# The first MLP of a two-layer block: both phases in a written order on all engines, weight differences kept in DRAM, row sums and row low parts on GpSimd

## The chip, the cores and the metric

The kernel runs on one core of one Trainium2 chip, as one launch. The metric is the device time in microseconds (us). The core has five engines: TensorE (PE; its weight loads are listed as PEld), VectorE (DVE), ScalarE (ACT), GpSimd (POOL) and SyncE (SP), which issues most of the DMAs. A difference under about 0.5% can't be told from none for this kernel.

## The reference, cut to what matters

Two layers over 512 latent tokens and 256 context tokens of width 1024. Layer 0 mixes tokens by pooling, layer 1 by attention; after each comes an MLP. The change is in the MLP of layer 0, which runs over all 768 tokens:

```python
def sq_relu_mlp(h, w_in, w_out):
    return jnp.square(jax.nn.relu(h @ w_in)) @ w_out

m_lat = sq_relu_mlp(modulate(rms_norm(x, g_mlp_pre[i]), sh2, sc2), w_mlp_in[i], w_mlp_out[i])
x = x + gt2 * rms_norm(m_lat, g_mlp_post[i])
```

`w_in` is 1024 x 4096, `w_out` 4096 x 1024, all float32. The context tokens go through the same weights with their own shift, scale and gate. Shifts, scales and gates of a layer come from `silu(cond) @ w_ada + b_ada`.

## The kernel before

**High and low parts.** A float32 product is made from three matmuls on rounded operands: high by high, high by low, low by high. The high part is a rounding copy on ACT (`sc.copy`), the low part a subtraction on DVE. Each operand therefore costs an ACT copy and a DVE subtraction ahead of its matmuls.

**First phase, class `Seven` (L819).** The hidden dimension of 4096 is cut into 16 groups of 256. Groups 2 to 15 are computed by a scheme of seven products in place of eight for a product of 2 x 2 blocks (Winograd's form of Strassen's scheme). The block sums of the rows are made once (`sums`), those of the weights for each group by `weights_sums` (L762), as six steps: casts on ACT, differences and low parts on DVE. A group's seven products are seven chains of 12 matmuls (128 x 128 by 128 x 384). Between the chains, banks of PSUM are copied by ACT to seed other sums, two DVE additions close the second half, and at the end two relus and two squares on ACT write the group's hidden rows into one of two buffers in `acc` (`hiddens`). `run(behind)` issues the pieces of other work (the next group's weight steps, the dots, the row sums) behind each chain.

**Row sums, `left_sums` (L981).** After each pair of groups, four sums of 768 elements per partition are made of their hidden rows on DVE, and seven tensors are written to `lefts` in DRAM through POOL's DMA queue. They are the left operands of the second phase. The hiddens of groups 14 and 15 are written to `ends` in DRAM.

**Dots.** Six tables of layer 1's and 0's conditioning are computed on DVE: a raw block of `w_ada` (1 MB) is loaded and multiplied with a broadcast row, with the sum in the accumulator (`ada_dot`, L343, 128 x 1024 elements). There are 24 blocks, 12 of them for two condition vectors (four dots), 12 for one (two dots). `ask` loads a block and queues its dots. The first phase takes 14 blocks; two go into the second phase; the last eight (`lone`) run in the stage behind the MLP's end, among the projections of the attention (`last0`).

**Second phase, `halves_` (L1054).** The seven-product scheme again, now on pairs of groups: 7 pairs, 7 products each, 49 products. A product is three row tiles of six matmuls (128 x 128 by 128 x 512), accumulated in PSUM over the 7 pairs. The products are grouped in passes, `PASSES = ((5, 3), (6, 4), (0, 1), (2,))`: a pass goes over all pairs for its one or two products, then `take` adds the banks to the result in `acc`. `load(j)` fetches weights and the row tensor of a product four ahead, `prepare(j)` makes weight differences and high and low parts two ahead. Products 3 to 6 need a difference of weight quarters; product 5 needs two, and product 3 starts from it.

**Order.** `TC_OPTS` has the build's planner order each engine's instructions by its own time estimates. `keep_in_program_order` pins an instruction to the written order of its engine. `Kept` is a wrapper that pins everything that an engine issues while its flag is set. Before, the matmuls of both phases are pinned (`mm`), the other engines are planned.

**Behind the MLP.** `finish` adds the products of groups 14 and 15 directly, then come norms, projections to keys, values and queries (`project`, L1380; `head_norm`, L1396 to L1410), the attention, and layer 1's MLP (`mlp1`).

Of the kernel before, what the change touches and what calls it, by code (L numbers as in the profile page):

```python
# [32 lines left out]
LATER, KEPT = 10, 8  # L33
# [65 lines left out]
def backbone(ctx: ExitStack, tc, x, ctx_in, w_ada, w_pool, w_qkv, g_q, g_k, w_o, w_mlp_in,  # L99
             w_mlp_out, vecs, rope, band, out):  # L100
    nc = tc.nc
    ordered, mixed = [False], [False]
    sy, gp = nc.sync, nc.gpsimd
# [31 lines left out]
    ends = dram.tile([P, 2, 2 * TOK], F32, name="ends")  # L135
# [676 lines left out]
    placed = [False]  # L812

    def mm(*args, **kw):
        z = te.matmul(*args, **kw)  # L815
        if placed[0]:
            tc.keep_in_program_order(z)

    class Seven:  # L819
# [3 lines left out]
        def chain(self, bank, n, start, stop):  # L823
            (wH, wL), (aH, aL) = self.products[n]
            for k in range(4):
                for m, (w, a) in enumerate(((wH, aH), (wH, aL), (wL, aH))):
                    mm(bank, w[k], a[k], start=start and k == 0 and m == 0, stop=stop and k == 3 and m == 2,
                       skip_group_check=True)

        def run(self, behind):  # L830
# [4 lines left out]
            for z in (b, c) if self.fresh else ():  # L835
                mm(z, wH[0], aH[0], start=True, stop=True, skip_group_check=True)
# [105 lines left out]
    def out_mm(i, parts, t, cols=HALVES):  # L942
# [12 lines left out]
        for n, h in order:  # L955
            a, f, w = seq[n]
            mm(pss[h][:, 0:cols[h][1]], a[:, f, ts_], w[:, f, cols[h][0]:sum(cols[h])],
               start=(n == 0 and not seeded[t]), stop=(n == len(seq) - 1), skip_group_check=seeded[t])
# [24 lines left out]
    def left_sums(p, even, odd):  # L983
# [3 lines left out]
        def one(n, d, a, b, op):  # L987
            ve.tensor_tensor(out=d, in0=a, in1=b, op=op)
# [16 lines left out]
    PASSES = ((5, 3), (6, 4), (0, 1), (2,))  # L1005

    def mlp0(inner, order, last, before_last):
# [18 lines left out]
        due = left_sums(0, early, hiddens[1])  # L1026
        sum_banks(True)
        placed[0] = True
        for g in range(2, NG):
            seven = Seven(products, hiddens[g % 2], (g + 1) % 2, g < 4)  # L1030
            pieces = []
            if g < NG - 1:
                steps, products = weights_sums(g + 1, raw)
                pieces += steps
                if g < NG - 2:
                    raw = raw_load(w_mlp_in[0, g + 2])
            if asked:
                pieces += asked.pop(0)
            if g % 2 == 0:
                pieces = due + pieces  # L1040
# [4 lines left out]
            for f in pieces[(7 * n + 3) // 7:]:  # L1045
                f()
            if g >= 2 * PAIRS:
                gp.dma_start(two(ends[:, g % 2]), hiddens[g % 2])
            elif g % 2:
                due = left_sums(g // 2, *hiddens)  # L1050
            if g == 4:
                head_gains()
        halves_(before_last)

    def halves_(before_last):
        todo = [(ps, p, n) for ps in range(len(PASSES)) for p in range(PAIRS) for n in PASSES[ps]]
        f, slots = S["f"], lambda z, w, n: [z[:, w * i:w * i + w] for i in range(n)]
        right = [f[:, 0:2048], f[:, 3584:5632]] + slots(ra, 2048, 6)
        left = [f[:, 2048:3584], rb[:, 0:1536]] + slots(f, 1536, 5) + slots(rb1, 1536, 2)
        uheld[0].close()  # L1060
        wide = uheld[0].enter_context(tc.tile_pool(name="wide", bufs=1)).tile([P, 8192], F32, name="wide")
        full = slots(wide, 2048, 4)
        arows = [slots(acc[:, 4 * TOK:], TOK, 4), slots(wide[:, 4096:], TOK, 5)]
        raws, sums_, ops, araw = {}, {}, {}, {}

        def home(slots, j):
            return slots[j] if j < 2 else slots[2 + (j - 2) % (len(slots) - 2)]

        def load(j):
            ps, p, n = todo[j]  # L1070
            raw = lambda: rawp.tile([P, 2048], F32, tag="raw", name="raw")
            if n == PASSES[ps][0]:
                f2 = lambda z: z.rearrange("p (f n) -> p f n", f=2)
                src = [f2(w_mlp_out[0, 2 * p + u]) for u in range(2)]
                z0 = full[(ps + p) % 2] if ps < 3 else raw()
                arow = z0[:, 1024:1024 + TOK]
                if ps == 3:
                    z0 = f2(z0[:, 0:1024])
                    sy.dma_start(z0, src[1][:, :, 512:])
                    raws[ps, p] = None, None, None, z0  # L1080
                elif ps == 2:
                    z0 = f2(z0)
                    for u in range(2):
                        sy.dma_start(z0[:, :, 512 * u:512 * u + 512], src[u][:, :, 0:512])
                    raws[ps, p] = z0[:, :, 0:512], None, z0[:, :, 512:], None
                else:
                    z0, z1 = f2(z0), f2(raw() if ps else full[2 + p % 2])
                    sy.dma_start(z0, src[0])
                    c = 512 if ps else 0
                    sy.dma_start(z1[:, :, c:], src[1][:, :, c:])  # L1090
                    raws[ps, p] = z0[:, :, 0:512], z0[:, :, 512:], z1[:, :, 0:512], z1[:, :, 512:]
            if ps < 3:
                z = arows[ps > 0]
                arow = z[(j + 4) % len(z)]
            araw[j] = arow
            sy.dma_start(arow, lefts[:, p, n])

        def prepare(j):
            ps, p, n = todo[j]
            b11, b12, b21, b22 = raws[ps, p]  # L1100
            tt = lambda d, a, b, op=ALU.subtract: ve.tensor_tensor(out=d, in0=a, in1=b, op=op)  # L1101
            if n in (0, 1, 2):
                b = (b11, b21, b22)[n]
            elif n == 3:
                b = sums_.pop(p)
                tt(b, b, b21)
            else:
                b = two(work_tile())
                tt(b, *((b12, b11), (b22, b12), (b22, b12))[n - 4])
                if n == 5:  # L1110
                    tt(b, b, b11, ALU.add)
                    sums_[p] = b
            r, l = home(right, j), home(left, j)
            wH, wL, aH, aL = two(r[:, 0:1024]), two(r[:, 1024:2048]), two(l[:, 0:TOK]), two(l[:, TOK:2 * TOK])
            sc.copy(wH, b)
            tt(wL, b, wH)
            a = two(araw.pop(j))
            sc.copy(aH, a)
            tt(aL, a, aH)
            ops[j] = wH, wL, aH, aL  # L1120

        where = lambda q, h, c: accv[:, 2 * q + h, 512 * c:512 * c + 512]
        add = lambda d, a, b, op=ALU.add: ve.tensor_tensor(out=d, in0=a, in1=b, op=op)

        def take(n, q, ps):
            c11, c12, c21, c22 = (where(q, h, c) for h in range(2) for c in range(2))
            if n == 5:
                sc.copy(c12, ps)
# [729 lines left out]
```

## Time and profile before

| what | us |
|---|---|
| median of 3 runs (1171.29 to 1175.4) | 1171.42 |
| the profiled execution | 1177.28 |
| its span, first to last instruction | 1175.5 |
| PE busy in the span (95%) | 1117.8 |
| DVE busy (79%) | 933.7 |
| ACT busy (53%) | 622.7 |
| POOL busy (9%) | 103.4 |

The profile is one execution. A row of a group gives the line, engine and operation, the tiles written and read, shapes and count, then the busy time and the mean duration in ns, then the engine's idle time ahead of it and what ended it. A row of a timeline gives start, duration, engine, line and operation, and in brackets the idle time before it and who ended that. PE's matmuls overlap: a row's duration is longer than the distance to the next start, so starts tell more than durations. A helper that records operations for its callers shows as one line, so L95 and L815 stand for many places; tile names tell them apart (`psin` first phase, `pso` second).

### The profile page before, as it was taken

What the parts mean: (1) busy time and instruction counts of PE and PEld (TensorE: products, weight loads), DVE (VectorE), ACT (ScalarE), POOL (GpSimd) and SP (SyncE); (2) the same over time, 40 slices, a digit from 0 to 9 for tenths busy, and PEclk for the clock granted to TensorE, in tenths of its full rate; (3) what the DMA queues carried; (4) which work ended last, traced back from release to release, by engine and by line L of the source; (5) the groups of instructions that cost most, each with busy time, mean ns of one, the idle gap of its engine ahead of it and who ended that gap; (6) DMA issues with size and microseconds to landing.
All of it is one profiled execution on the core that took longest, in us unless ns stands there. A gap on an engine that the chain in (4) does not pass through costs nothing. (4 is left out here: it accounts for less than half of the span.)

```text
span 1175.5 us, 15873 instructions
## 1 busy us (share of the span) xinstructions
PE 1117.8 (95%) x6030; PEld 971.2 (83%) x6030; DVE 933.7 (79%) x1332; ACT 622.7 (53%) x1038; POOL 103.4 (9%) x164
## 2 busy tenths in 40 slices
PE   7799799999979999999999899999999999999997
PEld 6479798999977778888887789998988888888886
DVE  5488888899859898757588889868687679778876
ACT  6387454555544454444385267762676346535523
POOL 1050111111100000000131310001100000000001
PEclk9799899999999999999999999999999999999999
DMA  9893576666699899627424602104434223214212
GB/s 371 287 386 130 188 242 216 209 223 221 230 354 354 305 387 351 206 88 258 160 90 151 243 1 72 37 9 189 154 115 152 76 95 144 108 37 143 108 33 112
DMA packets 48877, 212.62 MB, mean 181 GB/s; under 512 B 7104, under 2 KB 10000, under 8 KB 32160
## 3 DMA queue, kind: packets, MB, share of 16 engines
q1 hardware_dynamic: 43920, 190.76, 45.1%
q0 software_dynamic: 4880, 20.84, 4.6%
q8 instruction: 47, 0.77, 0.3%
q14 instruction: 30, 0.25, 0.1%
HBM read 183.40 MB, written 28.19 MB: 180 GB/s over the span
## 5 line engine op out<-in xcount | busy, mean ns | idle before, releaser
L815 PE MATMUL pso<-ra,sums 128*128 128x512 f32 x630 | 146.7, 393 | 4.7 <-DVE ra L1101 4.1
L815 PEld LDWEIGHTS pso<-ra,sums 128*128 128x128 f32 x630 | 119.1, 190 | 31.2 <-DVE ra L1101 5.4
L683 PE MATMUL psin<-ra,rb 128*128 128x512 f32 (+1 forms) x310 | 87.8, 360 | 0.0
L1256 PE MATMUL pso<-units,pairs 128*128 128x512 f32 x336 | 82.7, 389 | 0.0
L683 PE MATMUL psin<-ra 128*128 128x512 f32 (+1 forms) x256 | 76.5, 376 | 0.0
L1256 PEld LDWEIGHTS pso<-units,pairs 128*128 128x128 f32 x336 | 63.1, 188 | 13.1
L343 DVE CUSTOM_DVE_ANT_0 waste<-raw,crow 128x1024 f32<-128x1024 f32 x56 | 68.3, 1219 | 6.3 <-DMA raw<-in_w_ada 5.9
L815 PE MATMUL psin<-ra,units 128*128 128x384 f32 x340 | 65.9, 343 | 6.2 <-ACT work L694 6.2
L243 POOL TENSOR_SCALAR ms<-ss 128x1 f32<-128x1 f32 x15 | 9.7, 645 | 685.6 <-ACT junk L230 665.6
L1260 DVE TENSOR_TENSOR acc<-acc,pso 128x512 f32<-128x512 f32 x72 | 48.6, 681 | 26.3 <-PE pso L1256 26.3
L815 PEld LDWEIGHTS psin<-ra,units 128*128 128x128 f32 x340 | 61.7, 195 | 6.5 <-ACT work L694 6.5
L683 PEld LDWEIGHTS psin<-ra,rb 128*128 128x128 f32 x310 | 55.6, 189 | 8.7
L815 PE MATMUL psin<-sums,units 128*128 128x384 f32 x336 | 60.8, 334 | 0.9 <-ACT psin L838 0.9
L815 PEld LDWEIGHTS psin<-sums,units 128*128 128x128 f32 x336 | 58.4, 188 | 1.2 <-ACT psin L838 1.2
L683 PE MATMUL psin<-rb,rb 128*128 128x512 f32 (+1 forms) x155 | 55.9, 362 | 0.6 <-DVE rb L1740 0.6
L1380 PE MATMUL psq<-units,ra 128*128 128x512 f32 x216 | 53.8, 400 | 0.9 <-DVE rb L1480 0.9
L683 PEld LDWEIGHTS psin<-ra 128*128 128x128 f32 x256 | 47.1, 188 | 8.7
L815 PE MATMUL pso<-ra,rb 128*128 128x512 f32 x216 | 50.1, 390 | 0.0
L1380 PEld LDWEIGHTS psq<-units,ra 128*128 128x128 f32 x216 | 41.0, 193 | 9.8 <-DVE rb L1480 1.3
L683 PE MATMUL psin<-rb,ra 128*128 128x512 f32 (+1 forms) x128 | 48.1, 376 | 0.0
L815 PEld LDWEIGHTS pso<-ra,rb 128*128 128x128 f32 x216 | 40.5, 188 | 8.6 <-DVE ra L1101 0.3
L986 POOL DMA_DIRECT2D lefts<-acc x48 | 30.1, 627 | 189.3 <-ACT psin L838 108.3
(342 smaller groups left out, 2692.4 us busy)
## 6 DMA issues: line engine op xcount, KB each, us to landing
raw<-in_w_ada SPq DMA_DIRECT2D x48, 1024.0 KB, 7.4
raw<-in_w_mlp_in SPq DMA_DIRECT2D x32, 1024.0 KB, 5.3
wide<-in_w_mlp_out SPq DMA_DIRECT2D x21, 1024.0 KB, 7.4
lefts<-acc POOLq DMA_DIRECT2D x48, 384.0 KB, 6.2
raw<-in_w_mlp_out SPq DMA_DIRECT2D x18, 1024.0 KB, 5.2
wide<-lefts SPq DMA_DIRECT2D x28, 384.0 KB, 6.3
raw<-in_w_mlp_out SPq DMA_DIRECT2D x14, 512.0 KB, 6.4
wide<-in_w_mlp_out SPq DMA_DIRECT2D x14, 512.0 KB, 6.0
```

What stands on the lines that cost most here:

```text
L243: gp.tensor_scalar(out=ms[:, 0:1], in0=ss[:, parts - 1:parts], scalar1=rest, scalar2=EPS, op0=ALU.add, op1=ALU.add)
L343: ve.tensor_tensor_reduce(out=spare, in0=raw[:, D * b:D * b + D], in1=rows[c], scale=1.0, scalar=0.0, op0=ALU.mult, op1=ALU.add, accum_out ...
L683: te.matmul(ps[:, bank, o:o + ln], w[:, k, fs], rhs, start=start, stop=(k == KT - 1 and n == 2), skip_group_check=len(ks) < KT or self.paired)
L815: z = te.matmul(*args, **kw)
L986: keep = lambda n, z: gp.dma_start(two(lefts[:, p, n]), z)
L1256: te.matmul(ps, a, w, start=(m == 0), stop=(m == len(seq) - 1))
L1260: ve.tensor_tensor(out=M[n][:, t], in0=M[n][:, t], in1=ps, op=ALU.add)
L1380: te.matmul(ps, a[:, k, sl], w[:, k % 4, :], start=(k == 0 and n == 0), stop=(k == KT - 1 and n == 2))
```

## The change

- All five engines are pinned in both phases: SP and POOL are wrapped by `Kept` as well, and `pin` sets all flags. The pieces are dealt out by `(n*z + 6)//7` in place of `(n*z + 3)//7`.
- `left_sums` runs on POOL right after an odd group, not on DVE in the next one.
- `Seven` uses the other group of four PSUM banks for even and odd groups.
- `halves_` becomes the class `Halves`. Its first four loads and two preparations (`begin`, `prepare(0)`, `prepare(1)`) are issued in group 15. Then loads run five products ahead and preparations three.
- Passes are `((0, 4), (2, 5), (6, 3), (1,))`. The differences of products 4 and 5 are written to `halfway` in DRAM by POOL's queue and read back as inputs of products 5 and 3. `take` has fewer additions.
- The row low part of each second-phase product is subtracted on POOL.
- The hiddens of groups 14 and 15 stay in `acc` and are split there (`inner_rows`); `ends` goes. Their output weights are split in four portions (`last_weights`).
- All dots are asked for by the second phase's odd products 3 to 21; `lone` goes.

```diff
-    sy, gp = nc.sync, nc.gpsimd
+    sy, gp = Kept(tc, nc.sync, queued), Kept(tc, nc.gpsimd, queued)
...
         def one(n, d, a, b, op):
-            ve.tensor_tensor(out=d, in0=a, in1=b, op=op)
+            gp.tensor_tensor(out=d, in0=a, in1=b, op=op)
             keep(n, d)
-        return [lambda: (keep(0, a11), keep(1, a12), keep(3, a22), one(4, s1, a21, a22, ALU.add)),
-                lambda: one(5, s2, s1, a11, ALU.subtract), lambda: one(6, s3, a11, a21, ALU.subtract),
-                lambda: one(2, s4, a12, s2, ALU.subtract)]
+        keep(0, a11)
+        keep(1, a12)
+        keep(3, a22)
+        one(4, s1, a21, a22, ALU.add)
+        one(5, s2, s1, a11, ALU.subtract)
+        one(6, s3, a11, a21, ALU.subtract)
+        one(2, s4, a12, s2, ALU.subtract)
...
-    PASSES = ((5, 3), (6, 4), (0, 1), (2,))
+    PASSES = ((0, 4), (2, 5), (6, 3), (1,))
+
+    def pin(on):
+        for z in (ordered, mixed, queued):
+            z[0] = on
...
-        due = left_sums(0, early, hiddens[1])
         sum_banks(True)
-        placed[0] = True
+        pin(True)
+        left_sums(0, early, hiddens[1])
+        chain = Halves()
         for g in range(2, NG):
-            seven = Seven(products, hiddens[g % 2], (g + 1) % 2, g < 4)
+            seven = Seven(products, hiddens[g % 2], g % 2, g < 4)
...
-            if work and len(work) > LATER:
+            if g < NG - 2:
+                raw = raw_load(w_mlp_in[0, g + 2])
+            if g < NG - 1:
                 ask(*work.pop(0))
+            else:
+                chain.begin()
+                pieces += [lambda: None] * 2 + [lambda: chain.prepare(0), lambda: None, lambda: chain.prepare(1)]
             n = len(pieces)
-            seven.run(lambda z: [f() for f in pieces[(n * z + 3) // 7:(n * z + n + 3) // 7]])
...
+            seven.run(lambda z: [f() for f in pieces[(n * z + 6) // 7:(n * z + n + 6) // 7]])
+            if g % 2 and g < 2 * PAIRS:
+                left_sums(g // 2, *hiddens)
...
+        def prepare(self, j):
+            ps, p, n = self.todo[j]
+            a, b = self.raws[ps, p] if n != 3 else self.raws[n, p]
             if n in (0, 1, 2):
-                b = (b11, b21, b22)[n]
+                b = a
+            else:
+                w = two(work_tile())
+                x, y = {4: (b, a), 5: (a, b), 6: (a, b), 3: (a, b)}[n]
+                ve.tensor_tensor(out=w, in0=x, in1=y, op=ALU.subtract)
+                if n in (4, 5):
+                    gp.dma_start(two(halfway[:, n - 4, p]), w)
+                b = w
...
+            sc.copy(aH, a)
+            sc.copy(wH, b)
+            gp.tensor_tensor(out=aL, in0=a, in1=aH, op=ALU.subtract)
+            ve.tensor_tensor(out=wL, in0=b, in1=wH, op=ALU.subtract)
...
+            if n in (0, 4):
+                sc.copy(c11 if n == 0 else c12, ps)
+            elif n == 5:
+                add(c21, c11, ps)
+                add(c22, c21, c12)
+                add(c12, c22, self.banks[2][q])
+            elif n == 6:
+                add(c21, c21, ps)
+                add(c22, c22, ps)
             elif n == 3:
...
+                add(c21, c21, ps, ALU.subtract)
+            elif n == 1:
+                add(c11, c11, ps)
...
+            far, near, last_ = 5, 3, len(self.todo)
+            self.load(4)
+            self.prepare(2)
+            for j in range(last_):
+                ps, p, n = self.todo[j]
+                if j + far < last_:
+                    self.load(j + far)
+                self.multiply(j)
+                if j + near < last_:
+                    self.prepare(j + near)
...
+                if asked:
+                    for f in asked.pop(0):
+                        f()
+                if work and j % 2 and j > 2:
+                    ask(*work.pop(0))
...
-            for m, what in enumerate(work):
-                st.at(54 + 4 * m, lone, *what)
+            assert not work and not asked
```

More of the change, by code (lines that the diff above doesn't have):

```diff
@@ L826, in chain @@
                 for m, (w, a) in enumerate(((wH, aH), (wH, aL), (wL, aH))):
-                    mm(bank, w[k], a[k], start=start and k == 0 and m == 0, stop=stop and k == 3 and m == 2,
+                    te.matmul(bank, w[k], a[k], start=start and k == 0 and m == 0, stop=stop and k == 3 and m == 2,
                        skip_group_check=True)
@@ L1051, in mlp0 @@
             if g == 4:
                 head_gains()
[L1053 to L1071, printed above, removed]
-            if n == PASSES[ps][0]:
[L1073 to L1080, printed above, removed]
@@ new lines, in mlp0, with __init__, begin, load @@
+        chain.run()
+        pin(False)
+        sum_banks(False)
+        before_last()
+        finish(0, chain.parts, (4, 5, 0, 1, 2, 3), last0)
+    class Halves:
+        def __init__(self):
+            self.todo = [(ps, p, n) for ps in range(len(PASSES)) for p in range(PAIRS) for n in PASSES[ps]]
+            f, slots = S["f"], lambda z, w, n: [z[:, w * i:w * i + w] for i in range(n)]
+            self.slots = slots
+            self.right = [f[:, 0:2048], f[:, 3584:5632]] + slots(ra, 2048, 6)
+            self.left = [f[:, 2048:3584], rb[:, 0:1536]] + slots(rb1, 1536, 2) + slots(f, 1536, 5)
+            self.arows = slots(acc[:, 4 * TOK:], TOK, 4)
+            self.raws, self.sums, self.ops, self.arow, self.banks, self.parts = {}, {}, {}, {}, {}, []
+            self.full, self.n = [], 0
+        def begin(self):
+            for j in range(4):
+                self.load(j)
+        def load(self, j):
+            ps, p, n = self.todo[j]
+            at = lambda u, h: two(w_mlp_out[0, 2 * p + u])[:, :, 512 * h:512 * h + 512]
+            if n == PASSES[ps][0]:
+                z = self.full[self.n % 2] if self.full and ps < 3 else rawp.tile([P, 2048], F32, tag="raw", name="raw")
+                self.n += 1
+                a, b = two(z[:, 0:1024]), two(z[:, 1024:2048])
+                if ps == 0:
+                    z = two(z)
+                    sy.dma_start(z, two(w_mlp_out[0, 2 * p]))
+                    a, b = z[:, :, 0:512], z[:, :, 512:]
+                elif ps == 1:
+                    sy.dma_start(a, at(1, 1))
+                    sy.dma_start(b, two(halfway[:, 0, p]))
@@ L1081, in load @@
                 elif ps == 2:
[L1082 to L1085, printed above, removed]
-                else:
[L1087 to L1091, printed above, removed]
@@ L1154, in multiply @@
                 for m, (a, w) in enumerate(seq):
-                    mm(banks[n][q], a, w, start=(p == 0 and m == 0), stop=(p == PAIRS - 1 and m == len(seq) - 1),
-                       skip_group_check=True)
+                    te.matmul(self.banks[n][q], a, w, start=(p == 0 and m == 0),
+                              stop=(p == PAIRS - 1 and m == len(seq) - 1), skip_group_check=True)
                 if p == PAIRS - 1:
-                    take(n, q, banks[n][q])
-        far, near = 4, 2
@@ L1195, in halves_, with inner_rows, last_weights @@
-        placed[0] = False
-        sum_banks(False)
-        before_last()
-        finish(0, parts_, (4, 5, 0, 1, 2, 3), last0)
+                    self.take(n, q, self.banks[n][q])
+        def inner_rows(self, q):
+            hi, lo = (two(rb[:, 3072 * q + 1536 * z:3072 * q + 1536 * z + 1536]) for z in range(2))
+            sc.copy(hi, hiddens[q])
+            ve.tensor_tensor(out=lo, in0=hiddens[q], in1=hi, op=ALU.subtract)
+            self.parts.append((NG - 2 + q, (hi, lo)))
+        def last_weights(self, q, f):
+            w = work_tile()
+            sy.dma_start(w, w_mlp_out[0, NG - 2 + q][:, D * f:D * f + D])
+            hi, lo = (unit[2 - q][:, 2048 * z + D * f:2048 * z + D * f + D] for z in range(2))
+            sc.copy(hi, w)
+            ve.tensor_tensor(out=lo, in0=w, in1=hi, op=ALU.subtract)
+            if f:
+                self.parts[q] += ((two(unit[2 - q][:, 0:2048]), two(unit[2 - q][:, 2048:4096])),)
@@ L1491, in q_b @@
         head_norm(ps, r, 4, 0, t, q32[:, t, 512 * ch:512 * ch + 512])
-    def lone(i, m, j, nc_):
-        raw = raw_load(w_ada[i, m, j])
-        for b in range(2):
-            ada_dot(i, m, j, nc_, raw, [gate[:, 0, :]], gate[:, 1, :], b)
     def last0(st, n, t):
```

153 lines of the change are left out of this document (48 added, 105 removed).

## The prediction

> **What bounds the kernel now.** I read the table by stages first. Its columns are the stretch, its length, the busy time of PE, PEld, DVE, ACT and POOL with their instruction counts, the granted clock, the DMA share and GB/s.
>
> ```profile
> 125.50:345.40 219.90, 211.19 (x1180) 207.12 (x1180) 186.61 (x276) 114.21 (x179) 30.03 (x48) 0.98 0.67 237
> 345.40:363.70 18.30, 10.48 (x38) 7.99 (x37) 11.16 (x10) 6.35 (x8) 0.53 (x1) 0.81 0.96 369
> 363.70:563.20 199.50, 194.78 (x848) 159.66 (x847) 160.38 (x167) 93.71 (x106) 0.00 (x0) 0.99 0.75 270
> 404.00:420.00 16.00, 13.54 (x51) 10.73 (x52) 16.00 (x17) 11.46 (x16) 0.00 (x0) 0.89 0.98 370
> 599.70:685.00 85.30, 79.61 (x367) 65.08 (x365) 74.40 (x137) 43.64 (x123) 24.48 (x32) 0.98 0.47 167
> ```
>
> PE is the busiest engine everywhere, so the gain to be had is PE's pauses. A busy sum hides them, so I count starts in PE's timeline.
>
> ```profile
> 125.63 4.20 PE L815 MATMUL psin<-ra,units 128*128 128x384 f32 x14 [6.20 <-ACT work L694]
> 224.37 4.32 PE L815 MATMUL psin<-sums,units 128*128 128x384 f32 x24
> 228.53 2.24 PE L815 MATMUL psin<-ra,units 128*128 128x384 f32 x12
> 343.41 2.25 PE L815 MATMUL psin<-ra 128*128 128x384 f32 x12
> 353.01 0.80 PE L815 MATMUL pso<-sums 128*128 128x512 f32 x1 [7.35 <-ACT sums L1115]
> 354.27 5.69 PE L815 MATMUL pso<-sums 128*128 128x512 f32 x17 [0.46 <-DVE sums L1101]
> 359.80 4.24 PE L815 MATMUL pso<-sums,rb 128*128 128x512 f32 x18
> 363.88 0.61 PE L815 MATMUL pso<-ra,sums 128*128 128x512 f32 x2
> ```
> ```profile
> L815 PE MATMUL pso<-ra,sums x630: 388/389/628, 363.9 to 563.1; 128*128 128x512 f32 x158
> ```
>
> **Stage A** (the `Seven` loop): 24 matmuls, two chains of 12, take 228.53 - 224.37 = 4.16 us from start to start, so a chain takes 2.08, a group of seven 14.56, and 14 groups 203.8. They took from 125.63 to 345.66: 220.0. **16.2 us are pauses.** **The turn**: 345.66 to 353.01, 7.35 us without a matmul. **Stage B** (the halves): a product of 18 takes 363.88 - 359.80 = 4.08, 49 of them 199.9; from 353.01 to 563.5 (the last start and its 0.389) are 210.5, so **10.6 us too much**. Of these the first product has 2.7 (353.01 to 359.80 in place of 4.08; the granted clock is 0.81 there), and 7.9 come later. **Stage C** (projections): 85.3 - 79.6 = **5.7 us**. Together 39.9 us.
>
> The view of waits says who makes PE late, and for what that engine waits in turn (total, times, longest):
>
> ```profile
> PEld psin L815 <- ACT work L850: 9.3, 10, 3.0
> ACT units L772 <- DMA raw<-in_w_mlp_in: 25.8, 10, 5.3
> DVE work L1101 <- DMA wide<-in_w_mlp_out: 6.1, 2, 5.2
> PE pk L1476 <- DVE xr L1410: 3.3, 1, 3.3
> ```
>
> In A, PE waits for ACT's copy of the fifth chain (L850), which stands in ACT's queue behind casts that wait for loads and for DVE. At the turn, DVE waits for the first weights. In C, PE waits for DVE.
>
> **The change, part by part.** Prices, as groups by form:
>
> ```profile
> L988 DVE TENSOR_TENSOR acc<-acc 128x768 f32<-128x768 f32 x25 | 23.8, 951 | 0.0
> L343 DVE CUSTOM_DVE_ANT_0 waste<-raw,crow 128x1024 f32<-128x1024 f32 x52 | 63.4, 1220 | 6.3 <-DMA raw<-in_w_ada 5.9
> L1101 DVE TENSOR_TENSOR ra<-work,ra 128x1024 fp32r<-128x1024 f32 x25 | 30.2, 1216 | 1.1 <-ACT ra L1115 1.1
> L1101 DVE TENSOR_TENSOR sums<-wide,sums 128x768 fp32r<-128x768 f32 x20 | 19.0, 952 | 13.9 <-ACT sums L1118 13.9
> L1123 DVE TENSOR_TENSOR acc<-acc,pso 128x512 f32<-128x512 f32 x23 | 14.6, 678 | 6.7 <-PE pso L815 6.7
> L343 DVE CUSTOM_DVE_ANT_0 gate<-raw,gate 128x1024 f32<-128x1024 f32 x16 | 19.5, 1218 | 1.3 <-DMA raw<-in_w_ada 1.3
> L772 ACT CAST units<-work 128x1024 fp32r<-128x1024 f32 x13 | 13.6, 1046 | 5.3 <-DVE work L792 5.3
> L860 ACT ACTIVATE acc<-work 128x768 f32<-128x768 f32 x26 | 20.5, 836 | 0.1
> ```
>
> *Row sums to GpSimd.* 28 sums of 768 elements leave DVE: 23.8 us in the group of 25. What POOL takes for one, no row shows. The lower end is DVE's 0.95. The nearest POOL rows with many elements and few:
>
> ```profile
> 1.00 0.29 POOL masks.py:199 TENSOR_SCALAR_AFFINE_SELECT ident<-ident 128x128 f32<-128x128 f32 x1
> 161.52 1.46 POOL L986 DMA_DIRECT2D lefts<-acc x2 [11.62 <-ACT psin L838]
> 573.05 0.30 POOL L243 TENSOR_SCALAR ms<-ss 128x1 f32<-128x1 f32 x1 [225.03 <-ACT junk L230]
> 807.93 1.81 POOL L243 TENSOR_SCALAR ms<-ss 128x1 f32<-128x1 f32 x1 [108.25 <-ACT junk L230]
> 654.60 1.07 POOL L1389 TENSOR_TENSOR rs<-ms,nhalf 128x4 f32<-128x4 f32 x1
> ```
> ```profile
> 807.28 2.29 DVE L202 TENSOR_TENSOR rb<-raw,rb 128x2048 fp32r<-128x2048 f32 x1 [0.84 <-ACT rb L199]
> 654.73 0.68 DVE L1408 TENSOR_TENSOR work<-work,acc 128x512 f32<-128x512 f32 x1
> ```
>
> 128 elements of one input took 0.29, so 768 would take 1.74; with two inputs at that rate 3.5, the upper end. I take 1.7. Per pair of groups POOL then has four sums and seven DMA issues of about 0.73 (L986): 6.8 + 5.1 = 11.9 of 29.1 us, at the upper end 19. The first three sums read the even buffer, which the next even group's squares overwrite some 17 us later; at the upper end they end after 3 x 0.73 + 3 x (3.5 + 0.73) = 14.9. So POOL as an engine is free. (The Trainium skill, "GPSIMD Engine Reference", Elementwise — side-by-side cycle accounting, gives 4497 ns for a two-input sum of 2048 elements; scaled, an estimate of 1.7 us for 768, which leaves the sum as it is.)
>
> *The written order in A.* The copies follow their chain at once on ACT, so the 9.3 us can go; DVE's work for the next weights comes in fixed slices. But DVE is nearly full: 186.6 - 23.8 = 162.8 us, 11.6 per group, and in a fixed order it also waits twice per group for ACT's cast of a difference (1.05 each): 13.7 of 14.56. Only 0.9 us per group are left, so what comes late from a load or from ACT passes to PE. The bounds are a gain of 16.2 and none; I take half, **8 us**.
>
> *The turn.* Loads and two preparations go into group 15, on buffers whose products are past, and the last group now uses the other four PSUM banks, so product 0's are free. This removes 7.35 and the slow first product's 2.7. New: ACT first does the last group's two relus and two squares (four of about 0.8: 3.2), then product 1's casts (0.84 + 1.05), then DVE's low part (1.22): ready 6.3 after the turn, where product 0 ends at 4.08. About 2 us are lost: **8 us** gained, bounds 4 and 10. Two POOL stores and two reloads of the last hiddens go too; they lay beside other work.
>
> *Passes and halves in DRAM.* DVE loses 49 row low parts (0.952: 46.6), 7 of 35 differences (1.216: 8.5), 6 of 27 adds (0.678: 4.1), and gains 16 dots (1.22: 19.5): 160.4 falls to 120.7. POOL gets 49 x 1.7 = 83 plus 14 issues, of 200 us; even at 3.5 it is not full. Operands are prepared three products ahead, not two.
>
> ```profile
> raw<-in_w_ada SPq DMA_DIRECT2D x48, 1024.0 KB, 7.4
> ```
>
> New waits: POOL's store of a difference waits for DVE, and the product's row low part stands behind it; DVE waits in its row for a dot's load, which lands after 7.4 us and is called one to two products ahead (4 to 8 us), and the low parts of weights stand behind the dot; SP calls that load between those of the products, in three shared buffers, so a late dot makes later loads late. The lead of three products (12.2 us) covers one such delay of up to about 8 us, not several in a row. Against it stands traffic: the code's shapes give 69 MB in B, where 270 GB/s x 199.5 us = 53.9 MB moved. While dots are asked for (products 4 to 21, 73 us) a pair moves 1.05 MB of weights, 0.79 of rows, 0.52 of stored difference and 1.05 for dots: 3.41 MB in 8.16 us, 418 GB/s. The stretch 404 to 420 shows 370 at share 0.98. So loads fall behind by 73 x (418/370 - 1) = 9.5 us; three products' lead takes about 8 of it. Of the 7.9 us of pauses I count **2** as gained (bounds: 7.9 gained, 9.5 lost).
>
> *No dots in C.* 16 dots, 19.5 us of DVE, leave a stage in which PE waits 3.3 for DVE. **3 us**, bounds 0 and 5.7.
>
> **Sum.** 8 + 8 + 2 + 3 = 21 us. The profiled execution took 1177.28 (span 1175.5), 5.9 over the median of 1171.42 of the runs; the gains are differences, so I take them from the median: **1150 us**.
>
> **The rivals.**
>
> *DVE and GpSimd shut each other out* (slower). The one-element instruction of POOL took 1.81 us at 807.93 against 0.30 at 573.05, and ended 0.17 after DVE's two-input instruction (807.28 + 2.29 = 809.57): DVE holds POOL up. The other way round, DVE's two-input instruction at 654.73 ran its usual 0.68 inside POOL's of 654.60 to 655.67. For that I forecast no stop of DVE; but POOL read only four elements there. If DVE stands still for a whole sum, A's pair has 6.8 us more, less 2 x 0.9 of slack: 5 x 7 pairs = 35, so A takes 239, 19 more than before. In B, DVE's 120.7, its 28 waits for casts (29) and POOL's 83 make 233 in a row, 204 where POOL fits those waits; at 218, 7.5 more than before. With the turn's gap (-5.5) and C (-3) that is +18: **1189 us**. It decides from about 1 us of stop per row sum: (16.2/7 + 1.8)/4. The Trainium skill ("SBUF — State Buffer", Who interferes with whom) states this rule: of a VectorE instruction with two SBUF inputs and a GpSimd instruction that reads SBUF, the second waits until the first is through. The trace agrees for POOL; no run here shows it for DVE.
>
> *The loads set B's pace.* Nothing of the lateness is absorbed: B gives 9.5 back and gains nothing, **1162 us**. For it: share 0.98 where PE already paused at 404 to 420; against: dots are over by product 22, and then demand falls to 2.36 MB in 8.16 us, 289 GB/s.
>
> *The order doesn't do what it says.* A's pauses come from DVE's load and from ACT's 25.8 us of waits for loads, which no order removes; with nothing won in A, B and C and 4 us at the turn it is **1167 us**.
>
> **How the numbers follow.** Forecast 0.43, shut-out 0.33, loads 0.10, order 0.14. A difference under about 0.5% (5.9 us) can't be told from none. Faster by more: the forecast, the loads and 0.03 of the rest, 0.56. Within: most of the order case, 0.12. Slower: 0.32. The range reaches from 1137 (34 of the 39.9 us won) to 1198, some way above the shut-out's value; the upper end of 3.5 us per sum lies beyond it. The likeliest case's own range is 1137 to 1161.
>
> **What would show it.** A: groups 14.6 us apart and DVE's two-input durations unchanged (1.22) beside POOL's sums; right for the shut-out if they stretch to 2 or 3 us, and if even groups are longer than odd ones. POOL's price: 1.7 us for a sum of 768. The turn: under 3 us without a matmul. B: product starts 4.08 apart; waits of DVE or ACT on stored differences or rows in products 4 to 21 speak for the loads. C: no wait of PE for L1410. The forecast is wrong if DVE's busy time in A rises though 28 instructions left it.

## The result and the profile after

The changed kernel takes **1246.29 us** (median of four runs, 1245.81 to 1248.35), the kernel before 1172.9 beside it (four runs, 1171.29 to 1175.4). The ratio is 1.0627, with the interval 1.0601 to 1.0653: **slower by 6%**, where 1150 was forecast, and beyond the range.

First the stages, in the view of windows as before (length; busy time and instruction count of PE, PEld, DVE, ACT, POOL; granted clock; DMA share; GB/s). The rows are stage A, stage B, and a stretch of stage C at the same distance behind the end of B as the one shown of before.

```profile
121.90:386.00 264.10, 221.10 (x1166) 217.33 (x1167) 214.26 (x249) 114.60 (x180) 83.91 (x77) 0.90 0.55 196
386.00:639.90 253.90, 217.31 (x884) 168.97 (x883) 209.73 (x151) 96.28 (x112) 103.73 (x62) 0.97 0.79 279
676.00:762.00 86.00, 85.80 (x411) 71.39 (x410) 66.00 (x117) 50.40 (x144) 20.70 (x34) 1.00 0.18 62
```

The reader sees C nearly without a pause (85.80 of 86.00), and A and B far longer. DVE is busier than before, though many of its instructions have left: 249 instructions take 214.26 us in A, where 276 took 186.61 in a stretch of before. That is the sign of being wrong that the prediction names for itself.

All kernels below are compared by the same marks, read from PE's starts: A from the second chain of group 2 (the first matmul on `sums`) to the end of the last `psin` matmul, the turn from there to the first `pso` matmul, B from there to the first matmul behind the second phase (`psg`), and the rest. In us:

| kernel | ahead of A | A | turn | B | rest | span |
|---|---|---|---|---|---|---|
| before | 129.7 | 216.0 | 7.35 | 210.3 | 612.2 | 1175.5 |
| after | 121.8 | 264.4 | none | 253.9 | 604.7 | 1244.6 |
| difference | -7.9 | +48.4 | -7.5 | +43.6 | -7.5 | +69.1 |

Three places gained 23 us together; two lost 92. The groups by form show what became of DVE's and POOL's instructions in A and B (122 to 700 us; busy time, mean ns, idle time ahead):

```profile
L94 DVE TENSOR_TENSOR ra<-work,ra 128x1024 fp32r<-128x1024 f32 x34 | 81.5, 2396 | 42.7 <-ACT ra L94 42.7
L94 DVE TENSOR_TENSOR work<-raw 128x512 f32<-128x512 f32 x26 | 29.3, 1128 | 0.0
L94 DVE TENSOR_TENSOR units<-raw,units 128x1024 fp32r<-128x1024 f32 x13 | 23.1, 1777 | 4.8 <-ACT units L94 4.8
L94 DVE CUSTOM_DVE_ANT_0 waste<-raw,crow 128x1024 f32<-128x1024 f32 x52 | 63.6, 1224 | 1.4
L94 POOL TENSOR_TENSOR sums<-wide,sums 128x768 fp32r<-128x768 f32 x28 | 54.0, 1943 | 28.8 <-ACT sums L94 28.6
L94 POOL TENSOR_TENSOR acc<-acc 128x768 f32<-128x768 f32 x25 | 46.2, 1846 | 0.5
```

Low parts of weights that took 1216 ns take 2396 on average (the 7 in A keep 1225, the 27 in B, beside POOL's low parts, take 2700), differences of weights 1128 (684 in the kernel with fills, below); the dots of A, which mostly lay outside POOL's sums, keep their 1224. One such burst in A, from the timelines of POOL, DVE, ACT and PE of the changed kernel (start, duration, what it is, in brackets the wait ahead):

```profile
202.85 1.89 POOL L94 TENSOR_TENSOR acc<-acc 128x768 f32<-128x768 f32 x1
205.75 1.85 POOL L94 TENSOR_TENSOR acc<-acc 128x768 f32<-128x768 f32 x1
208.59 1.81 POOL L94 TENSOR_TENSOR acc<-acc 128x768 f32<-128x768 f32 x1
211.30 1.82 POOL L94 TENSOR_TENSOR acc<-acc 128x768 f32<-128x768 f32 x1
...
203.08 1.70 DVE L94 TENSOR_TENSOR mods<-mods,vec 128x16 f32<-128x16 f32 x1
204.70 1.21 DVE L94 TENSOR_TENSOR units<-raw,units 128x1024 fp32r<-128x1024 f32 x1
205.84 2.31 DVE L94 TENSOR_TENSOR work<-raw 128x512 f32<-128x512 f32 x1
208.06 2.37 DVE L368 TENSOR_TENSOR gc<-mods,vec 128x8 f32<-128x8 f32 x2
210.36 0.68 DVE L94 TENSOR_TENSOR work<-raw,work 128x512 f32<-128x512 f32 x1
...
211.08 1.04 ACT L94 CAST units<-work 128x1024 fp32r<-128x1024 f32 x1 [8.08 <-DVE work L94]
212.03 0.47 ACT L94 COPY psin<-psin 128x384 f32<-128x384 f32 x1
...
212.55 0.69 PE L94 MATMUL psin<-sums,rb 128*128 128x384 f32 x1 [5.97 <-ACT psin L94]
214.32 2.44 PE L94 MATMUL psin<-sums,rb 128*128 128x384 f32 x7
...
230.44 1.39 PE L94 MATMUL psin<-sums,ra 128*128 128x384 f32 x7
```

Read from the bottom: PE waits 5.97 us for ACT's copy from bank to bank; that copy stands in ACT's written queue behind a cast, which has waited 8.08 us for DVE's difference; and DVE stood still while POOL summed. The difference of 205.84, called just behind POOL's sum of 205.75, ends at 208.15, 0.55 after that sum (207.60): it stood for the sum and then ran. Its low part at 204.70 took its usual 1.21, because it began as the first sum ended (204.74); POOL's next sum began only behind its DMA issue, at 205.75. After the pause seven matmuls take 2.44 us where seven take 1.39 otherwise, so that each pause costs more than its length; the granted clock of the stage is 0.90.

PE at the turn, as a timeline:

```profile
383.94 2.24 PE L94 MATMUL psin<-ra 128*128 128x384 f32 x12
386.02 4.49 PE L94 MATMUL pso<-sums 128*128 128x512 f32 x18
390.83 0.49 PE L94 MATMUL pso<-sums,rb 128*128 128x512 f32 x1 [0.31 <-ACT sums L94]
392.87 3.47 PE L94 MATMUL pso<-sums,rb 128*128 128x512 f32 x14 [1.55 <-DVE sums L94]
```

The first product starts 2.08 us after the last chain, so the turn has no pause. And the waits of B (386 to 640 us; total, times, longest), then the one of A that counts, from the view of the whole span:

```profile
DVE ra L94 <- ACT ra L94: 34.1, 30, 1.4
PE pso L94 <- DVE ra L94: 29.9, 25, 2.7
DVE units L94 <- DMA work<-in_w_mlp_out: 6.4, 1, 6.4
DVE sums L94 <- ACT sums L94: 4.0, 2, 2.9
...
PE psin L94 <- ACT psin L94: 42.4, 8, 6.4
```

In B, DVE's 209.73 us of busy time and its waits of 34.1, 6.4 and 4.0 make 254.2 of the 253.9: **DVE is the engine that bounds B.** PE waits for it in about every second product.

### The profile page after: what moved, and what is told of

The parts are those of the page before. It is cut to its first block, busy times and chain, and to the rows that moved or that the text cites. A ratio compares the mean times of both kernels' runs of the same rounds, so it can differ in the third digit from the quotient of the medians.

```text
span 1244.6 us, 15869 instructions
## 1 busy us (share of the span) xinstructions
PE 1138.9 (92%) x6030; PEld 982.9 (79%) x6030; DVE 980.3 (79%) x1242; ACT 616.5 (50%) x1035; POOL 255.0 (20%) x253
## 4 chain that ended last, share of the span: by engine, by line
PE 54%; DVE 22%; issue 9%; ACT 7%; DMA 4%; POOL 3%; SPq 0%; ACTq 0%; POOLq 0%; DVEq 0%
PE psin L682 14%; PE pso L1261 11%; PE psin L94 8%; DVE work L94 7%; DVE ra L94 5%; PE pso L949 4%; PE psq L1385 4%; DVE waste L94 3%; PE psy L1669 3%; PE po L1645 3%; DVE units L94 3%; PE pss L1604 3%; DMA raw<-in_w_ada 2%; ACT ra L94 2%; ACT units L94 2%
## 5 line engine op out<-in xcount | busy, mean ns | idle before, releaser
L94 PEld LDWEIGHTS pso<-ra,sums 128*128 128x128 f32 x594 | 113.5, 194 | 55.9 <-DVE ra L94 25.2
L94 DVE TENSOR_TENSOR ra<-work,ra 128x1024 fp32r<-128x1024 f32 x34 | 81.5, 2396 | 42.7 <-ACT ra L94 42.7
L94 ACT CAST ra<-work 128x1024 fp32r<-128x1024 f32 x34 | 35.6, 1046 | 135.0 <-DVE work L94 124.3
L94 DVE CUSTOM_DVE_ANT_0 waste<-raw,crow 128x1024 f32<-128x1024 f32 (+1 forms) x72 | 89.6, 1245 | 1.7
L94 PE MATMUL pso<-ra,rb 128*128 128x512 f32 x252 | 63.9, 408 | 10.9 <-DVE ra L94 10.9
L94 PEld LDWEIGHTS pso<-ra,rb 128*128 128x128 f32 x252 | 48.8, 197 | 24.8 <-DVE ra L94 14.3
L94 PE MATMUL psin<-sums,rb 128*128 128x384 f32 x70 | 27.8, 539 | 42.0 <-ACT psin L94 42.0
L94 POOL TENSOR_TENSOR sums<-wide,sums 128x768 fp32r<-128x768 f32 x28 | 54.0, 1943 | 28.8 <-ACT sums L94 28.6
L94 PEld LDWEIGHTS psin<-sums,rb 128*128 128x128 f32 x70 | 22.3, 327 | 44.2 <-ACT psin L94 44.2
```

What stands on the lines that cost most here:

```text
L94: return lambda *args, **kw: self.tc.keep_in_program_order(f(*args, **kw))
```

## The experiments

### POOL's two parts taken back, one at a time and together

The edits to the changed kernel:

```diff
 # sums_dve and both_dve: left_sums
-            gp.tensor_tensor(out=d, in0=a, in1=b, op=op)
+            ve.tensor_tensor(out=d, in0=a, in1=b, op=op)
 # lows_dve and both_dve: Halves.prepare
-            gp.tensor_tensor(out=aL, in0=a, in1=aH, op=ALU.subtract)
+            ve.tensor_tensor(out=aL, in0=a, in1=aH, op=ALU.subtract)
 # memset: in both places, instead of the sum
+            for _ in range(3):
+                gp.memset(...)
```

> Only the row sums of the first phase go back to VectorE, in one burst of four right behind an odd group; row low parts stay on GpSimd. Shut-out: stage A falls by 35-55 us, stage B stays at about 254; 1190-1212 us. Order theory: the burst of four sums stays in the way, A stays over 250 and the time over 1230.

> Only the row low parts of the second phase go back to VectorE. Shut-out: stage B falls by 35-50 us to 205-218, stage A stays at about 267; 1195-1212 us. Load theory: stage B hardly moves, over 240; over 1230 us. A gain of this run and of the row sums' run that add up to the gain of both speaks for two separate causes, one for each stage.

> The changed kernel with its row sums and its row low parts back on VectorE; the written order, the passes and the differences in DRAM stay. Shut-out theory (VectorE stands still while GpSimd reads two inputs): the 77 sums of about 1.9 us no longer stop VectorE; stage A falls from 267 to 205-222 us, stage B from 254 to 203-215, the whole to 1150-1175 us. Order theory (the written order on all engines costs by itself, whoever makes the sums): stages A and B stay over 240 each and the time stays over 1220. Load theory (traffic sets stage B): stage B stays over 240, A falls, about 1200.

> Each sum on GpSimd is replaced with three fills of the same tile with zero (768 elements each; an estimate from the fill of 128 elements in 0.20 us and of one in 0.10 is about 0.7 us each, 2.1 for three), so the row sums and the row low parts are left out, while GpSimd is about as busy and the stores keep their places. Shut-out by reading: fills read nothing, VectorE's 1024-element subtraction is back at 1.22 us and the time is 1145-1170 us. If GpSimd as a busy or late engine (or its writing) is what costs, the time stays over 1220 us and VectorE's instructions stay stretched.

| kernel | us | ratio to before, interval | A | B |
|---|---|---|---|---|
| sums_dve | 1230.41 | 1.0454 [1.0436, 1.0471] | 248.8 | 253.3 |
| lows_dve | 1199.38 | 1.0189 [1.0173, 1.0205] | 264.1 | 208.5 |
| both_dve | 1184.86 | 1.0063 [1.0045, 1.0081] | 249.9 | 208.3 |
| memset | 1149.53 (one run) | | 215.3 | 204.8 |

The low parts cost B 45 us, as the shut-out has it. The fills keep POOL busy in the same places and read nothing from SBUF; windows of A and B and groups of that kernel:

```profile
124.30:339.60 215.30, 206.85 (x1167) 201.88 (x1168) 169.40 (x251) 114.71 (x180) 94.82 (x135) 1.00 0.65 231
339.40:544.20 204.80, 201.16 (x884) 165.39 (x883) 139.54 (x150) 97.93 (x112) 112.87 (x158) 1.00 0.92 350
```
```profile
L94 DVE TENSOR_TENSOR ra<-work,ra 128x1024 fp32r<-128x1024 f32 x34 | 41.7, 1226 | 43.6 <-ACT ra L94 43.6
L94 DVE TENSOR_TENSOR work<-raw 128x512 f32<-128x512 f32 x26 | 17.8, 684 | 0.0
L94 POOL MEMSET sums<- 128x768 f32 x102 | 75.0, 743 | 20.8 <-PE pso L94 13.9 <-DMA acc<-lefts 3.0
```

DVE's durations are the old ones (1226, 684), with POOL busy for 94.82 us in A. So it isn't that POOL works, but that it reads. **The price of the stop**, as an average: in A (214.26 - 169.40) / 29 = 1.55 us each (28 sums and the first low part), in B (209.73 - 139.54) / 48 low parts = 1.46. (The expectations further down divide by 28 and 49, and so have 1.6 and 1.43.) It isn't a constant, as runs further down show.

But A did not behave as the shut-out alone would have it: with the sums on DVE it still takes 249.9, 34 more than before, and the sums account for only 15 of the 48 us. A second cause was open there.

### How much POOL has to read

```diff
-            gp.tensor_tensor(out=d, in0=a, in1=b, op=op)
+            gp.tensor_copy(out=d, in_=a)
 # and aL likewise: gp.tensor_copy(out=aL, in_=a)
```

> The changed kernel with each of GpSimd's 28 sums and 49 low parts replaced by one copy of the first operand (one input from SBUF in place of two; it leaves out the row sums and the row low parts). If any instruction of GpSimd that reads SBUF stops VectorE: its two-input instructions beside a copy stretch by the copy's length, and the run lies between 1180 and 1246 us by that length. If only two-input instructions of GpSimd do so: VectorE's durations stay at 1.22 us, first phase 215, second 205, the run about 1149 as with fills.

1174.74 us, ratio 1.0005 [0.9983, 1.0027]; A 236.4, B 209.7. Its groups:

```profile
L94 DVE TENSOR_TENSOR ra<-work,ra 128x1024 fp32r<-128x1024 f32 x34 | 57.0, 1677 | 44.8 <-ACT ra L94 44.8
L94 POOL CAST sums<-wide 128x768 fp32r<-128x768 f32 x28 | 23.6, 862 | 27.6 <-DMA wide<-lefts 24.0 <-PE pso L94 3.6
```

DVE's low part is 0.45 us longer than beside fills, with copies of 0.86. A copy that reads one operand stops DVE too. The total lies slightly below the band of 1180 to 1246 that was expected of this theory, and far from the 1149 of the other. The Trainium skill ("SBUF — State Buffer", Who interferes with whom) puts it so: a VectorE instruction with two inputs from SBUF contends with a GpSimd instruction that reads SBUF, and not with one that only writes. The three kernels agree: 2.40 us beside sums, 1.68 beside copies, 1.23 beside fills.

### The second cause: the written order of A

Why does A take 249.9 with no sum on POOL? Its window first, then the timelines of DVE, ACT and PE of both_dve, at one even group:

```profile
122.40:372.40 250.00, 221.05 (x1167) 217.28 (x1168) 195.55 (x280) 115.39 (x181) 30.02 (x48) 0.92 0.59 208
```
```profile
233.85 3.68 DVE L94 TENSOR_TENSOR acc<-acc 128x768 f32<-128x768 f32 x4
...
239.30 0.69 DVE L94 TENSOR_TENSOR work<-raw,work 128x512 f32<-128x512 f32 x1
...
240.03 1.04 ACT L94 CAST units<-work 128x1024 fp32r<-128x1024 f32 x1 [6.16 <-DVE work L94]
240.98 0.47 ACT L94 COPY psin<-psin 128x384 f32<-128x384 f32 x1
...
241.51 0.45 PE L94 MATMUL psin<-sums,rb 128*128 128x384 f32 x1 [4.04 <-ACT psin L94]
```

DVE is busy for 195.55 of 250 us, so it has time left. The timelines show the same chain as with POOL: the four sums stand ahead of the weight difference, the cast waits 6.16 us for it, the bank copy stands behind the cast, PE pauses 4.04. So theory Q: ACT's written queue carries DVE's delay to PE, and the place of the pieces decides. Theory L: DVE has too much to do in A, and no order helps. Four kernels:

```diff
 # late_dve (on both_dve), late_pool (on the changed kernel): groups before the last
+                home_, d1, t_, d2, t34, b22_, *dots = pieces
+                dealt = [[home_, d1], [d2], [t_], [t34], [b22_], dots[:1], dots[1:]]
-            seven.run(lambda z: [f() for f in pieces[(n * z + 6) // 7:(n * z + n + 6) // 7]])
+                seven.run(lambda z: [f() for f in dealt[z]])
 # spread_late besides (the sums of left_sums as four pieces, `due`)
+                if g % 2 == 0:
+                    for z in range(4):
+                        dealt[1 + z].append(due[z])
 # spread_dve: the even group's pieces, dealt out as in the change
+                pieces[3:] = [pieces[3], due[0], pieces[4], due[1], pieces[5], due[2], due[3]] + pieces[6:]
```

> Row sums and row low parts on VectorE as in both_dve (1184.86 us, first phase 249.9 us); only the place of the next group's weight steps differs: the second difference is issued behind chain 1, the cast of the first difference behind chain 2, after ScalarE's PSUM copy, and so on one chain later. Theory Q (ScalarE's written queue carries VectorE's delay to PE, because the copy stands behind a cast that waits): the eight waits of about 4 us (28 us) go, the first phase falls to about 222 us, the run to 1150 to 1162. Theory L (VectorE simply has too much to do in the first phase, whatever the order): the pauses move to another place, the first phase stays at 240 to 250 and the run above 1175.

> As both_dve, but the four row sums of a pair are pieces between the next even group's weight steps (behind chains 2 to 5) in place of a burst ahead of them; the casts keep their places. Theory Q, in the form that it is the burst ahead of the difference which makes the cast late: the first phase falls to 216 to 225 us (the value without any sums was 215.3), the run to 1150 to 1162. Theory L: first phase 240 to 250, run above 1175.

> Both edits together: row sums one behind each of chains 1 to 4 of the next even group, and the first cast after the PSUM copy. Theory Q: no pause over 1 us in the first phase, 206 to 215 us for it (203.8 needed by the matmuls), the run 1140 to 1150, below both kernels. Theory L: 235 or more, the run above 1165.

> The changed kernel (1246.3 us, first phase 264.4) with row sums and low parts on GpSimd as it has them; only the weight steps stand one chain later, with the first cast after the PSUM copy. If the stop of VectorE by GpSimd's sums reaches PE only through ScalarE's queue at that cast (theory Q), the first phase falls to 220 to 235 us and the run to 1202 to 1218, the second phase staying at 254. If the time that VectorE loses in the burst (theory L) cannot be made up in the rest of the pair, the first phase stays above 250 and the run above 1230.

| kernel | us | ratio to before, interval | A | B |
|---|---|---|---|---|
| late_dve | 1162.99 | 0.9906 [0.9884, 0.9928] | 225.3 | 208.9 |
| spread_dve | 1168.60 | 0.9949 [0.9928, 0.9969] | 231.5 | 208.6 |
| spread_late | 1152.89 | 0.9819 [0.9799, 0.9839] | 215.9 | 209.7 |
| late_pool | 1246.79 | 1.0617 [1.0595, 1.0638] | 264.2 | 253.7 |

With all work on DVE theory Q holds: the same instructions in other places take A from 249.9 to 215.9, and each of the two edits alone does part of it (all three runs came out 1 to 7 us above the band given for Q). The window of A of spread_late, with no pause left that slows PE's clock:

```profile
123.50:339.40 215.90, 208.77 (x1167) 201.74 (x1168) 192.49 (x280) 115.99 (x180) 30.02 (x48) 1.00 0.67 237
```

With POOL summing theory Q fails: late_pool gains nothing, A is as long as in the changed kernel. Its waits show why:

```profile
PE psin L94 <- ACT work L94: 47.1, 7, 7.2
```

The pause has moved one step on, from the bank copy to ACT's copies into the work tiles, once per pair and as long as before. DVE is busy for 225.0 us of A here. That its loss in a burst is too large to be hidden by the place of a single cast fits this, but no run shows it by itself.

### The written order of A taken away

```diff
 # planned_a (on both_dve): in A only PE is pinned
+        for z in (ordered, mixed, queued) if on != "PE" else (ordered,):
-        pin(True)
+        pin("PE")
 ...
+        pin(True)
         chain.run()
```

> The kernel both_dve (1184.9 us; first phase 249.9), with only PE held to the written order in the first phase and the other four engines planned there, as in the kernel before; the second phase stays written. If the written order of those engines makes the 34 us by which its first phase is longer than before: first phase 214 to 222 us, the run 1148 to 1160. If they come from the other things that differ from before in this phase (the row sums called directly behind the odd group, the banks by turns, the dots asked for in other groups), the first phase stays above 235 and the run above 1168.

**1143.51 us, ratio 0.9720 [0.9685, 0.9756]**, the fastest kernel of the study, below the band expected of the first theory. Windows of A and B:

```profile
125.30:332.30 207.00, 205.82 (x1167) 205.18 (x1168) 190.47 (x281) 120.68 (x182) 30.10 (x48) 0.98 0.71 249
332.10:538.30 206.20, 203.11 (x884) 167.55 (x884) 175.95 (x194) 93.86 (x108) 6.96 (x13) 0.98 0.91 343
```

The same pieces with DVE, ACT, POOL and SP planned take 207 us, 43 less than written out (249.9), with DVE about as busy (190.47 against 195.55). So DVE was not too full; the order was the cause. PE's wait for the bank copy that stood behind the cast is gone; first the row of both_dve, then that of planned_a:

```profile
PE psin L94 <- ACT psin L94: 28.3, 8, 4.5
PE psin L94 <- ACT psin L836: 0.5, 1, 0.5
```

A is 9 us shorter than in the kernel before, too; which of the remaining differences does that (the banks by turns, the groups in which dots are asked for) was not tried apart.

### GpSimd's parts alone, in the planned order of before

```diff
 # b_sums_pool, on the kernel before: left_sums
-            ve.tensor_tensor(out=d, in0=a, in1=b, op=op)
+            gp.tensor_tensor(out=d, in0=a, in1=b, op=op)
 # b_lows_pool, on the kernel before: prepare
-            tt(aL, a, aH)
+            gp.tensor_tensor(out=aL, in0=a, in1=aH, op=ALU.subtract)
```

> The kernel before with one edit: its row sums on GpSimd, in the planner's order. VectorE's busy time in the first phase (186.5 us of 220) loses 26 us of sums and, by the stop theory, gains 28 stops of about 1.6 us (that is 214.3 - 169.4 over 28, the changed kernel against the one with fills): about 206. With its waits for casts that is more than the 220: first phase 228 to 245 us, the run 1183 to 1200. If the loss in the first phase belongs to the written order alone, the planner works round the stops: first phase 215 to 222, the run 1168 to 1178.

> The kernel before with one edit: the row low part of each product of the second phase on GpSimd, in the planner's order. Stop theory: VectorE's 169 us in the second phase lose 47 and gain 49 stops of 1.43 us (209.7 - 139.3 over 49), 70: about 192 of 210, and with its waits for casts the phase goes to 225 to 245 us (210.3 before), the run to 1187 to 1207. If the written order is needed for the loss: 205 to 212 us for the phase, the run 1166 to 1177.

b_sums_pool 1201.20, ratio 1.0220 [1.0175, 1.0266], A 247.5 where before has 216.0; b_lows_pool 1203.46, ratio 1.0221 [1.0176, 1.0267], B 231.5 where before has 210.3. The windows of A of the first and of B of the second:

```profile
130.10:377.60 247.50, 218.04 (x1167) 209.53 (x1166) 210.17 (x247) 113.88 (x176) 79.00 (x73) 0.96 0.58 209
354.60:586.20 231.60, 214.77 (x883) 173.15 (x884) 185.28 (x127) 95.79 (x110) 110.65 (x47) 0.94 0.70 248
```

Either part costs some 2% by itself, with only PE's matmuls in a written order. The low parts cost B less than in the changed kernel (21 us in place of 45); the passes and the lead of the preparations differ too, so these runs don't say what softens it. The sums cost A 31. The first of these runs came out just above its band (1200), the second within it.

### One burst, or the sum of the stops

```diff
 # pool_spread: spread_late with the sums on POOL
-            ve.tensor_tensor(out=d, in0=a, in1=b, op=op)
+            gp.tensor_tensor(out=d, in0=a, in1=b, op=op)
 # pool_paced: besides, ahead of the second to fourth sum
+            for _ in range(0 if n == 4 else 2):
+                gp.memset(d, 0.0)
```

> The kernel spread_late (1152.9 us; first phase 215.9, VectorE busy 192.5 in it) with only the row sums on GpSimd, one behind each of four chains in place of a burst. Stop theory: each sum stops VectorE for 1.6 us in place of the 0.95 it costs there: VectorE at about 211 of 216 before its waits, first phase 228 to 245, the run 1165 to 1182. If only the burst of four sums does the harm, and single sums fit between VectorE's instructions: first phase 212 to 220, the run 1148 to 1157.

> The kernel pool_spread (1200.2 us; first phase 264.4, where GpSimd ran its four sums in one go all the same, because nothing held it back) with two fills of about 0.75 us, which do not stop VectorE, ahead of the second, third and fourth sum, so that the four sums lie over some 15 us in place of 10. If the closeness of the stops makes the loss (each pair's slack is used between the sums): first phase 235 to 252 us, the run 1171 to 1188. If only their total counts (28 times 1.6 us): first phase 259 to 267, the run 1195 to 1204.

pool_spread: 1200.23, ratio 1.0212 [1.0181, 1.0243], A 264.4, worse than either theory had it. I had written the sums behind four chains, but nothing held POOL back: it ran them in one go as soon as the hidden rows were there, and PE's longest waits in A are those of late_pool, number for number (47.1 us in 7 waits for ACT's work tiles). The stops are dearer here: against the 169.4 us of DVE with fills, (226.0 - 169.4) / 28 = 2.0 us each. pool_paced: 1177.39, ratio 1.0023 [1.0004, 1.0042], A 239.1. The windows of A, of the first and of the second:

```profile
121.90:386.40 264.50, 216.36 (x1167) 213.46 (x1168) 226.00 (x252) 115.60 (x181) 81.86 (x76) 0.91 0.56 196
```
```profile
122.90:361.90 239.00, 217.07 (x1167) 212.27 (x1168) 209.78 (x252) 115.77 (x180) 117.93 (x118) 0.95 0.59 215
```

POOL does more (118 us for 82), and A is 25 us shorter: with the sums further apart, less is lost. Two things change at once, though. DVE's own time falls from 226.0 to 209.8, because a paced sum stops it for only (209.8 - 169.4) / 28 = 1.4 us; that is 16 us of DVE's time. Whether the rest comes from the distance between the stops was not tried apart. The sums still cost 23 us against spread_late's 215.9.

## Why the prediction was wrong, point by point

**The step that failed first: "I forecast no stop of DVE".** It rested on one row, in which POOL's instruction read four elements a partition. Sums of 768 stop DVE for 1.55 us each on average, above the break-even of 1 us that the prediction named for itself: 45 us of DVE's time in A and 70 in B, which the forecast had at nothing. The rival had the right mechanism (shown by sums against copies against fills), and it was given less chance than the forecast on the weaker row.

**The rival's size was off as well**, 1189 against 1246. For B it had DVE at 120.7 us without stops, its 28 waits for casts and POOL's 83 in a row as a worst case of 233, and chose 218. The runs show 139.5 without stops, 70 of stops and 44.5 of waits, 254: DVE's own load was set too low (8.7 us of it because the 160.4 that it starts from is the stretch from 363.7 on, without B's first products; from 353.0 DVE has 169.07), and 70 of POOL's 103.73 us (its DMA issues among them) came on top of it, however many waits there were to fit them in. For A it forecast 239 on marks that take in the first chain; on these 267 were measured (118.99 to 386.18), because of the next point.

**The step that failed second: "the written order in A" as a gain between 0 and 16.2 us.** Its lower bound was wrong. As written, the order costs 43 us (249.9 against 206.9 planned, with the sums on DVE in both). The prediction counted DVE's slack as a mean, 0.9 us per group, and missed that a queue in written order hands on the worst moment: four sums, 3.68 us in a row, ahead of a difference, a cast that waits for it, and a bank copy behind that cast. The sentence that the copies follow their chain at once on ACT does not hold for the one behind that cast. (The sum also takes off 23.8 us, the row of 25 sums, for 28, which would be 26.6; that is 0.2 us a group and changes nothing.)

**The two losses overlap in A.** Both run through the same cast. Against both_dve the sums on POOL cost 14.5 us, pool_spread's against spread_late 48.5, and in the planned order of before 31.5: what the sums cost depends on what is there to hide their stops.

**POOL's price**, 1.7 us, was near: 1.85 for a row sum, 1.94 for the largest group of low parts (2.25 in the slowest).

**The turn** came out as forecast, 8 us: the gap of 7.35 is gone; the first product takes 4.81 us from start to start, where 2.7 too much were counted before and now 0.73; 1.55 are lost at the second product. 7.35 + 2.0 - 1.55 = 7.8.

**Passes and halves in DRAM**: 2 us of gain were forecast, and 43.6 were lost, through the stops. Where nothing stops DVE, B takes 206.2 to 209.7 (planned_a, both_dve, spread_late), 0.6 to 4.1 us less than before. That agrees with the 2 in size only: these kernels have the low parts on DVE, and the term had taken them off it. As the cause of the loss the loads are out: 343 GB/s moved in planned_a, 350 with fills, where B took 204.8.

**No dots in C**: 3 us forecast, bounds 0 to 5.7. The rest behind B is 7.5 shorter, and the shown stretch of C went from 5.7 us of pauses to 0.2, close to the upper bound; some 2 us more went outside the stretch.

**Ahead of A** 7.9 us were gained that the prediction didn't count: the wait of 6.20 us for ACT's work tile at 125.63 is gone. Why was not tried by itself; it is gone in every kernel built on the change.

So the forecast of 1150 comes near only to the change without its GpSimd part and without the written order in A: that kernel, planned_a, takes 1143.5, a gain of 32 us where 21 were forecast. The nearness bears out none of the terms that rested on those two parts: A gains 9 there with the sums on DVE and the order planned, and 4.3 ahead of A and 8.2 behind B, where 0 and 3 were forecast, come from elsewhere.

## What to carry to other kernels

Before work is moved to GpSimd to relieve VectorE, price it as time that VectorE loses: in these runs a GpSimd sum of 768 elements, which VectorE does in 0.95 us, stopped VectorE for 1.4 to 2.0, so the move made the busy engine busier, and only fills, which read nothing, left its two-input instructions alone. A written order is to be judged by its longest chain of waits across queues, not by an engine's mean load: look for an instruction that PE needs at once (a bank copy) standing behind one that may wait (a cast of weights for the next group). And listing a piece behind a chain paces it only on an engine that has something to wait for there.

## What was not expected of the hardware

- The stop does not scale with the stopped instruction: VectorE's instruction on 128 x 16 took 1.70 us beside a sum of GpSimd's (203.08 above), and two on 128 x 8 took 2.37. A stop can also be longer than the sum is by its record: of those two the first took 0.15 and the second 2.30, from about 208.1, when POOL was issuing a DMA, to 210.43, where the sum of 208.59 (1.81) ends.
- Casts on VectorE with one input were held up in the kernel with fills as well, where two-input instructions kept their times. In its timeline, two casts of 8 elements and, behind them, two two-input instructions of the same size:

```profile
193.64 1.31 DVE L392 CAST gh<-gc 128x8 fp32r<-128x8 f32 x2
194.98 0.24 DVE L393 TENSOR_TENSOR gh<-gc,gh 128x8 fp32r<-128x8 f32 x2
```

The casts took 1.31 us where two like instructions take 0.24, and 0.16 each in the kernel before. POOL issued a DMA from 193.60 and began fills at 194.16. Which of these holds the casts was not tried.
- PE's slow stretch behind a pause: in both_dve a pause of 4.04 us was enough for it (seven matmuls behind it take 2.38 us, and the granted clock of A is 0.92 there, 1.00 in spread_late), so a pause of four to six microseconds costs more than it shows.
